# Query and key transfers of a hybrid decoder's mixer: transfers with an outermost DRAM dimension of two replaced by transfers of 32 or 64 rows

## The chip, the core and the metric

One core of a Trainium2 chip runs the whole program. The metric is device microseconds of one execution, as the median of several runs; less is better.

## What is computed

Two decoder layers over 512 tokens of width 1024, all in float32. Each layer is a half-step SwiGLU FFN, a token mixer and a second half-step FFN, each followed by a layer norm. The mixer makes one input projection, hands its columns to three groups of heads, and projects their outputs back:

```python
aq, ak, av, bq, bk, bv, cc = jnp.split(x @ w_in[l], IN_SPLIT_IDX, axis=-1)
...
o_a = diff_attention(rope(aq), rope(ak), av, lam)      # 6 heads, two 32-wide score maps each
...
o_b = dilated_attention(rope(bq), rope(bk), bv)        # 6 heads of width 64
...
o_c, v_first = rwkv7_mixer(cc, ...)                    # 4 heads, a scan over the tokens
mix = jnp.concatenate([o_a, o_b, o_c], axis=-1) @ w_out[l]
x = layer_norm(DEEPNORM_ALPHA * x + mix, ...)
```

## The kernel before

Every large product is made of three matmuls of rounded halves (hi times hi, hi times lo, lo times hi), so that TensorE (PE) carries most of the time. The FFNs run over tiles of 128 tokens and 512 columns, with weights streamed through a ring (lines 70 to 87). The change lies in the mixer, which runs once in each of the two layers, from about 390 to 860 us and from about 1536 to 2010 us of the profiled execution.

In the mixer some twenty generators each write one strand of the work. A planner (`Board`, lines 369 to 479) keeps a modelled time for each engine and merges the strands: it always takes the strand whose next step is ready by the model, in the order of a list of ranks, and so sets the order of the instructions on every engine. The engines then work through their queues in that order. Its model gives a DMA issued by GpSimd (POOL) 1.04 us on POOL, and then the time of the bytes and 2 us more. Nothing in the model depends on the shape of a transfer. Most mixer instructions carry line 511, the line of the planner's wrapper, so they are told apart by the names of their tiles.

The strands that matter here:

- `columns` computes the input projection in 13 parts (p<-wh,xhi, p<-wl,xhi, p<-wh,xlo, 128x256). It is ready early and long, and the planner fills PE with it where attention isn't ready; below it is called the filler.
- `weights` loads the raw columns (wr, by SyncE), rounds them on ScalarE (wh) and subtracts on POOL (wl); eight wh and eight wl tiles hold two parts.
- `turner` transposes the rotated queries and keys (m<-kept,rc), splits them into hi and lo (z) and stores them to DRAM: qkA and qkB, three tensors each, one for a pair of heads, laid out as [hi or lo, q or k, 128 channels, 512 tokens].
- `fetch` (line 766) brings one head after another back into SBUF, by POOL's DMAs. A head takes two tiles, q and k, of four such slots, so two heads are in flight, and the next head's transfers wait for the last scores of the head before the last. The first head of each group also loads the group's bias tile, for which there is one slot: group B's waits until VectorE (DVE) has read A's for the last time.
- `attend` makes the scores of one head in four units of 128 queries (A: two matmuls p<-k,q each, on 96 rows; B: p<-q on 128 rows and p<-k,q on 64), then softmax on DVE and ScalarE (ACT), transposes (m<-kept,t) and products with the values (r<-v,aT).
- `inside`, `invert`, `scan` and `rwkv_out` do the RWKV heads, with many small matmuls of 64 or 32 columns.

A head of group A (heads are numbered pair, half) needs 96 rows of 4 KB in each tile, in q the rows hi, lo, hi and in k the rows hi, hi, lo. Rows 0 to 63 came by one transfer per tile, with a DRAM pattern of two by 32 rows: outermost step 256*S for q, and step 0 for k, which reads the same rows twice. Rows 64 to 95 came by a transfer of 32 rows. A head of group B took q's 128 rows by two transfers of two by 64 rows of 2 KB, and k2 by one of 64 rows.

Of the kernel before, what the change touches and what calls it, by code (L numbers as in the profile page):

```python
# [16 lines left out]
S = 512  # L17
# [349 lines left out]
HALF = [slice(0, 64), slice(64, 128)]  # L367
# [153 lines left out]
class Mix:  # L521
# [247 lines left out]
    def fetch(self):  # L769

        dma = self.gps.dma_start
        ap = lambda t, off, dims: bass.AP(tensor=t.tensor, offset=t.offset + off, ap=dims)
        for grp in "AB":
            for hp in range(3):
                for e in range(2):
                    yield f"qk{grp}{hp}", "x", "x"
                    if (hp, e) == (0, 0):
                        yield f"qk{grp}{hp}", "x", "x", "bias"
                        self.bias = self.get("bias", "bias")
                        dma(self.bias, self.tr.consts[:, 130:642] if grp == "A" else self.tr.consts[:, 642:1154])  # L780
                    a = self.get("x", "q", (128, 2, S))
                    d = self.qk[grp, hp]
                    hi, lo, k = e * 64 * S, (256 + e * 64) * S, 128 * S
                    if grp == "A":
                        b = self.get("x", "k", (128, 2, S))
                        dma(a[0:64], ap(d, hi, [[256 * S, 2], [2 * S, 32], [1, 2 * S]]))
                        dma(b[0:64], ap(d, hi + k, [[0, 2], [2 * S, 32], [1, 2 * S]]))
                        dma(a[64:96], ap(d, hi, [[2 * S, 32], [1, 2 * S]]))
                        dma(b[64:96], ap(d, lo + k, [[2 * S, 32], [1, 2 * S]]))
                    else:  # L790
                        b = self.get("x", "k2", (64, S))
                        dma(a[:, 0, :], ap(d, hi, [[256 * S, 2], [S, 64], [1, S]]))
                        dma(a[:, 1, :], ap(d, hi + k, [[0, 2], [S, 64], [1, S]]))
                        dma(b, ap(d, lo + k, [[S, 64], [1, S]]))
                    self.qkt[grp, hp, e] = a.bitcast(FR), b.bitcast(FR)
                    self.mark(f"q{grp}{hp}{e}")
# [753 lines left out]
```

## Time and profile before

| | |
|---|---|
| median of 3 runs | 2329.84 us (2324.28 to 2331.13) |
| the profiled execution, its own time | 2319.83 us |
| its span, first to last instruction | 2318.0 us |
| PE busy | 2215.6 us, 96% of the span |
| DVE, ACT, POOL busy | 1146.8, 803.4, 317.5 us |
| mean granted TensorE clock | 0.975 of 2.4 GHz |
| chain of waits that ended last: PE, DVE, DMA | 80%, 8%, 5% |

The page puts the busy time of each engine, its waits, the granted clock and the DMA queues beside each other. The waits of PE tell which transfers or engines it stood still for. The granted clock of a stretch tells at which of its two levels (1.2 and 2.4 GHz) the matmuls in it ran: 0.50 is the lower one, 1.00 the upper.

### The profile page before, as it was taken

To read this page: it belongs to the slowest core of one execution; us is meant where nothing else is said; L and a number is where in the kernel's file an instruction comes from. 1 tells how busy PE (TensorE), PEld (TensorE's weight loads), DVE (VectorE), ACT (ScalarE), POOL (GpSimd) and SP (SyncE) were. 2 spreads that over 40 slices of the span, in tenths; PEclk is the share of its full clock that TensorE was granted. 3 is DMA by queue.
4 is the path that set the end of the run, shared out by engine and by line. 5 is a ranking of instruction groups with operands and counts; after the bars stand their busy time and mean duration, and the time that the engine had idled before them with its cause. 6 is when DMAs were issued, how large, how long until landed. Compare 5 with 4: busy or idle time off the path is not lost.

```text
span 2318.0 us, 31736 instructions
## 1 busy us (share of the span) xinstructions
PE 2215.6 (96%) x12384; PEld 1863.6 (80%) x12384; DVE 1146.8 (49%) x2483; ACT 803.4 (35%) x1559; POOL 317.5 (14%) x344
## 2 busy tenths in 40 slices
PE   9999999988899999999999999999878999999998
PEld 8888888787776788888888888887877867888886
DVE  3333346766566633333653332656765666333336
ACT  4322223435444323222433222343444443222222
POOL 1000002343232200000010000033432322000000
PEclk9999999999899999999999999999987999999999
DMA  5333344354433323332543333432553323233334
GB/s 171 101 102 98 113 137 146 102 136 98 104 106 101 118 74 94 98 99 91 173 120 108 101 96 109 155 128 85 136 108 94 107 95 119 84 98 91 100 109 154
DMA packets 253030, 258.34 MB, mean 111 GB/s; under 512 B 45562, under 2 KB 202304, under 8 KB 252880
## 3 DMA queue, kind: packets, MB, share of 16 engines
q1 hardware_dynamic: 221488, 228.20, 32.4%
q0 software_dynamic: 30816, 27.06, 4.8%
q8 instruction: 97, 1.59, 0.3%
q10 hardware_dynamic: 576, 1.05, 0.1%
q14 instruction: 53, 0.43, 0.1%
HBM read 233.85 MB, written 22.28 MB: 110 GB/s over the span
## 4 chain that ended last, share of the span: by engine, by line
PE 80%; DVE 8%; DMA 5%; issue 4%; POOL 1%; ACT 1%; SPq 0%; POOLq 0%; DVEq 0%; ACTq 0%
PE p L87 18%; PE p L86 18%; PE p L85 18%; PE p L511 13%; PE m L511 4%; PE r L511 3%; DMA k<-qkA 3%; PE r L86 2%; PE r L85 2%; PE r L87 2%; DMA k<-qkB 1%; DVE x L511 1%; POOL wl L511 1%; DMA q<-qkB 0%; DVE x L146 0%
## 5 line engine op out<-in xcount | busy, mean ns | idle before, releaser
L80 DVE TENSOR_TENSOR lo<-raw,hi 128x1024 fp32r<-128x1024 f32 x300 | 366.2, 1223 | 627.8 <-ACT hi L79 627.5
L87 PE MATMUL p<-xhi,lo 128*128 128x512 f32 (+1 forms) x1392 | 535.7, 385 | 0.0
L86 PE MATMUL p<-xlo,hi 128*128 128x512 f32 (+1 forms) x1392 | 533.7, 383 | 0.7 <-DVE xlo L126 0.7
L85 PE MATMUL p<-xhi,hi 128*128 128x512 f32 (+1 forms) x1392 | 533.6, 383 | 0.5 <-ACT xhi L125 0.5
L79 ACT CAST hi<-raw 128x1024 fp32r<-128x1024 f32 x300 | 315.6, 1053 | 583.5 <-PE p L86 258.1
L86 PEld LDWEIGHTS p<-xlo,hi 128*128 128x128 f32 x1392 | 261.7, 188 | 56.3 <-DVE xlo L126 1.1
L85 PEld LDWEIGHTS p<-xhi,hi 128*128 128x128 f32 x1392 | 261.8, 188 | 53.8 <-ACT xhi L125 1.0
L87 PEld LDWEIGHTS p<-xhi,lo 128*128 128x128 f32 x1392 | 261.9, 188 | 52.6
L511 POOL TENSOR_TENSOR wl<-wr,wh 128x512 fp32r<-128x512 f32 x152 | 203.8, 1360 | 670.1 <-ACT wh L511 629.3
L511 PE MATMUL p<-wh,xhi 128*128 128x256 f32 (+1 forms) x704 | 233.7, 332 | 1.4 <-DVE rb L511 1.1
L511 PE MATMUL p<-wh,xlo 128*128 128x256 f32 (+1 forms) x704 | 218.9, 311 | 0.5 <-DVE xlo L511 0.4
L511 PE MATMUL p<-wl,xhi 128*128 128x256 f32 (+1 forms) x704 | 218.5, 310 | 0.0
L87 PE MATMUL p<-hi,hl 128*128 128x512 f32 x528 | 205.8, 390 | 0.0
L86 PE MATMUL p<-lo,hh 128*128 128x512 f32 x528 | 205.8, 390 | 0.0
L85 PE MATMUL p<-hi,hh 128*128 128x512 f32 x528 | 205.7, 390 | 0.0
L511 PEld LDWEIGHTS p<-wh,xhi 128*128 128x128 f32 x704 | 138.9, 197 | 12.7 <-PE p L511 1.5
L511 PEld LDWEIGHTS p<-wh,xlo 128*128 128x128 f32 x704 | 138.7, 197 | 7.6 <-DVE xlo L511 2.2
L246 DVE TENSOR_TENSOR hr<-p,hr 128x512 f32<-128x512 f32 x88 | 60.8, 691 | 167.3 <-PE p L87 156.9
L511 PEld LDWEIGHTS p<-wl,xhi 128*128 128x128 f32 x704 | 139.2, 198 | 4.3
L247 ACT CAST hh<-hr 128x512 fp32r<-128x512 f32 x88 | 54.3, 617 | 205.9 <-DVE hr L246 195.8
L511 ACT ACTIVATE t<-t,nm 128x128 f32<-128x128 f32 (+3 forms) x144 | 80.2, 557 | 125.0 <-DVE nm L511 124.0
L85 PEld LDWEIGHTS p<-hi,hh 128*128 128x128 f32 x528 | 99.1, 188 | 20.6
(253 smaller groups left out, 3061.0 us busy)
## 6 DMA issues: line engine op xcount, KB each, us to landing
raw<-in_ffn_a_down SPq DMA_DIRECT2D x66, 512.0 KB, 3.3
raw<-in_ffn_b_down SPq DMA_DIRECT2D x66, 512.0 KB, 3.3
raw<-in_ffn_a_gate SPq DMA_DIRECT2D x44, 512.0 KB, 3.8
raw<-in_ffn_a_up SPq DMA_DIRECT2D x44, 512.0 KB, 3.9
raw<-in_ffn_b_gate SPq DMA_DIRECT2D x40, 512.0 KB, 3.9
raw<-in_ffn_b_up SPq DMA_DIRECT2D x40, 512.0 KB, 3.8
wr<-in_w_in SPq DMA_DIRECT2D x56, 256.0 KB, 3.1
wr<-in_w_in SPq DMA_DIRECT2D x24, 512.0 KB, 3.8
```

The source lines that it names most:

```text
L79: nc.scalar.copy(hi, raw)
L80: (vec or nc.vector).tensor_tensor(lo, raw, hi.bitcast(FT), op=OP.subtract)
L85: mm(out, lh, rh, start=first, stop=False)
L86: mm(out, lh, rl, start=False, stop=False)
L87: mm(out, ll, rh, start=False, stop=last)
L246: nc.vector.tensor_tensor(hr, acc[1, f], hr, op=OP.mult)
L247: nc.scalar.copy(hi, hr)
L511: return call(*args, **kw)
```

## The change

In group A each of the two transfers of 64 rows becomes two of 32 rows, so that a head takes six transfers of 32 rows in the place of four. In group B each of the two transfers of 128 rows becomes two of 64, so that a head takes five in the place of three. Bytes and destinations stay as they are. For 12 heads in two layers that is 48 DMAs more on POOL's queue.

```diff
                     if grp == "A":
                         b = self.get("x", "k", (128, 2, S))
-                        dma(a[0:64], ap(d, hi, [[256 * S, 2], [2 * S, 32], [1, 2 * S]]))
-                        dma(b[0:64], ap(d, hi + k, [[0, 2], [2 * S, 32], [1, 2 * S]]))
-                        dma(a[64:96], ap(d, hi, [[2 * S, 32], [1, 2 * S]]))
-                        dma(b[64:96], ap(d, lo + k, [[2 * S, 32], [1, 2 * S]]))
+                        for n, (q, r) in enumerate(((hi, hi), (lo, hi), (hi, lo))):
+                            rows = slice(32 * n, 32 * n + 32)
+                            dma(a[rows], ap(d, q, [[2 * S, 32], [1, 2 * S]]))
+                            dma(b[rows], ap(d, r + k, [[2 * S, 32], [1, 2 * S]]))
                     else:
                         b = self.get("x", "k2", (64, S))
-                        dma(a[:, 0, :], ap(d, hi, [[256 * S, 2], [S, 64], [1, S]]))
-                        dma(a[:, 1, :], ap(d, hi + k, [[0, 2], [S, 64], [1, S]]))
+                        for rows, q in zip(HALF, (hi, lo)):
+                            dma(a[rows, 0, :], ap(d, q, [[S, 64], [1, S]]))
+                            dma(a[rows, 1, :], ap(d, hi + k, [[S, 64], [1, S]]))
                         dma(b, ap(d, lo + k, [[S, 64], [1, S]]))
```

The planner prices each added DMA at 1.04 us of POOL and so merges the strands in another order, on all engines and in both layers alike. Three places of the first layer show how.

POOL's queue at the fetch of group B's first pair of heads, before (bias, q and k are the tiles that the DMAs fill, wl the rounded remainders of the weights):

```order
L511 TENSOR_TENSOR wl<-wr,wh 128x512 x4
L511 DMA bias<-in_constants 128x512
L511 DMA q<-qkB_0_2687 128x1x512 x2
L511 DMA k_5615<-qkB_0_2687 64x512
L511 DMA q<-qkB_0_2687 128x1x512 x2
L511 DMA k_5620<-qkB_0_2687 64x512
L511 TENSOR_TENSOR wl<-wr,wh 128x512 x8
```

and after:

```order
L511 TENSOR_TENSOR wl<-wr,wh 128x512 x8
L511 DMA bias<-in_constants 128x512
L511 DMA q<-qkB_0_2687 64x512 x4
L511 DMA k_5604<-qkB_0_2687 64x512
L511 DMA q<-qkB_0_2687 64x512 x4
L511 DMA k_5611<-qkB_0_2687 64x512
L511 TENSOR_TENSOR wl<-wr,wh 128x512 x4
```

Each head has two transfers more, and four subtractions of weights have moved from behind the fetch to ahead of it.

PE's queue at the first two units of head (1,0) of group A, before (p<-wh,xlo and p<-wh,xhi are filler; the numbers behind p only count tiles):

```order
L511 MATMUL p_4492<-wh,xlo 128x256
L511 MATMUL p_4539<-k,q 128x256
L511 MATMUL p_4545<-k,q 128x256
L511 MATMUL m<-kept,t 128x128 x3
L511 MATMUL r<-v,aT 128x64 x2
L511 MATMUL p_4492<-wh,xhi 128x256
```

and after:

```order
L511 MATMUL p_4591<-wh,xlo 128x256
L511 MATMUL r<-t_4302,x_4306 32x32 x16
L511 MATMUL r<-t16t,x_4306 32x32 x16
L511 MATMUL p_4643<-k,q 128x256
L511 MATMUL p_4649<-k,q 128x256
L511 MATMUL m<-kept,t 128x128 x3
L511 MATMUL r<-v,aT 128x64 x2
L511 MATMUL p_4676<-k,q 128x256
L511 MATMUL p_4682<-k,q 128x256
```

Between the last scores of head (0,1) and these first ones there were 24 filler matmuls and three batches of the RWKV inversion, and now there are 54 and four. In return the second unit follows the first without the 12 filler matmuls that stood between them.

PE's queue at the start of group B, before:

```order
L511 MATMUL r<-v,aT 128x64 x4
L511 MATMUL m<-uv,am 64x64 x4
L511 MATMUL r<-t16t,x_4449 32x32 x16
L511 MATMUL p_5753<-q 128x256
L511 MATMUL p_5753<-k_5615,q 128x256
L511 MATMUL p_5761<-q 128x256
L511 MATMUL p_5761<-k_5615,q 128x256
L511 MATMUL m<-uv,am 64x64
```

and after:

```order
L511 MATMUL r<-uv,am 64x64
L511 MATMUL r<-st,kr 64x64
L511 MATMUL p_5790<-q 128x256
L511 MATMUL p_5790<-k_5604,q 128x256
L511 MATMUL p_5798<-q 128x256
L511 MATMUL p_5798<-k_5604,q 128x256
L511 MATMUL r<-zs,t16t 64x64 x4
L511 MATMUL m<-uv,am 64x64
```

From the last scores of group A to these first ones of group B there were 24 filler matmuls, and now there are 72. In return the eight units of B's first two heads, among which 48 filler matmuls were spread, now have none.

## Rows read from the trace of the kernel before

**Rows 1.** The page: busy us, share of the span and instructions, by engine.
```profile
PE 2215.6 (96%) x12384; PEld 1863.6 (80%) x12384; DVE 1146.8 (49%) x2483; ACT 803.4 (35%) x1559; POOL 317.5 (14%) x344
```

**Rows 2.** PE's waits, whole span: us in total, times, longest.
```profile
PE p L511 <- DMA k<-qkA: 38.7, 6, 11.5
...
PE p L511 <- DMA q<-qkB: 1.7, 2, 1.2
```

**Rows 3.** PE's timeline at score matmuls: start, us; in brackets the idle time before.
```profile
506.02 0.76 PE L511 MATMUL p<-k,q 96*128 96x256 f32 x2 [3.50 <-DMA k<-qkA]
...
545.05 0.77 PE L511 MATMUL p<-k,q 96*128 96x256 f32 x2 [8.60 <-DMA k<-qkA]
...
588.54 0.77 PE L511 MATMUL p<-k,q 96*128 96x256 f32 x2 [6.03 <-DMA k<-qkA]
...
630.72 0.55 PE L511 MATMUL p<-q 128*128 128x256 f32 x1 [1.23 <-DMA q<-qkB]
```

**Rows 4.** POOL's timeline at fetches: start, us of the issues; in brackets POOL's wait.
```profile
492.56 0.69 POOL L511 DMA_DIRECT2D q<-qkA  x1 [1.57 <-issue]
...
526.40 0.72 POOL L511 DMA_DIRECT2D q<-qkA  x1
...
574.15 0.70 POOL L511 DMA_DIRECT2D q<-qkA  x1
...
618.06 0.59 POOL L511 DMA_DIRECT2D bias<-in_constants  x1 [12.11 <-DVE r L511]
618.78 1.63 POOL L511 DMA_DIRECT2D q<-qkB  x2
620.38 0.59 POOL L511 DMA_DIRECT2D k<-qkB  x1
```

**Rows 5.** Single DMAs: size, us to landing (issued at 618.06, 618.78 and 494.42).
```profile
bias<-in_constants POOLq DMA_DIRECT2D x1, 256.0 KB, 2.8
...
q<-qkB POOLq DMA_DIRECT2D x1, 256.0 KB, 11.6
...
k<-qkA POOLq DMA_DIRECT2D x1, 128.0 KB, 11.4
```

**Rows 6.** POOL's DMA queue, 707 to 711 and 721 to 724 us: packets, MB, share.
```profile
q0 software_dynamic: 163, 0.37, 25.5%
...
q0 software_dynamic: 303, 1.11, 98.5%
```

**Rows 7.** The page: reloads of x by POOL, count, size, median us to landing.
```profile
x<-x POOLq DMA_DIRECT2D x8, 512.0 KB, 4.3
```

**Rows 8.** Filler, then eight stretches after waits: window, length, PE busy (instructions), granted clock, DMA.
```profile
496.00:500.00 4.00, 4.00 (x36) 1.00 0.92 184
...
506.00:512.00 6.00, 5.98 (x38) 0.74 0.45 69
545.00:553.00 8.00, 7.95 (x65) 0.68 0.20 61
588.50:597.00 8.50, 8.46 (x62) 0.65 0.09 26
628.00:644.00 16.00, 14.77 (x91) 0.57 0.21 56
1658.60:1665.00 6.40, 6.34 (x39) 0.73 0.43 70
1700.70:1709.00 8.30, 8.29 (x60) 0.61 0.14 46
1743.80:1757.00 13.20, 13.18 (x86) 0.58 0.10 31
1785.00:1801.00 16.00, 15.76 (x98) 0.57 0.23 55
```

**Rows 9.** 40 us of group B: PE, PEld, DVE, ACT, POOL busy, granted clock, DMA, GB/s.
```profile
700.00:740.00 40.00, 35.88 (x217) 27.05 (x216) 27.26 (x129) 20.80 (x74) 9.61 (x14) 1.00 0.38 123
```

**Rows 10.** What POOL waited for, 480 to 720 us.
```profile
POOL wl L511 <- ACT wh L511: 102.4, 11, 28.1
```

## The prediction

> **What bounds the kernel now.** I read the busy times first: PE works in 96% of the span [rows 1], so time can only come out of PE's own standing still, or out of its clock. Next come PE's waits, longest in total first. At the head stands not an engine but a transfer: the keys of group A, 38.7 us in six waits of up to 11.5 us, and with the queries of group B 40.4 us [rows 2]. PE's timeline places them: three A waits in each layer, at the first scores of a head. In the first layer PE came to them at 502.5, 536.5, 582.5 (A) and 629.5 us (B) and went on at 506.0, 545.1, 588.5 and 630.7 [rows 3]. POOL's timeline shows the other end: the transfers of these heads were issued from 492.56, 526.40, 574.15 and 618.78 [rows 4], so they landed 12 to 18 us after the first issue. A last look goes to the granted clock behind each wait: 0.57 to 0.74 over the next 6 to 16 us, where plain filler runs at 1.00 [rows 8]. PE comes back from standing still at 1.2 GHz. A stretch of length L at mean clock c loses L times (1 - c): behind the six A waits 1.6 + 2.6 + 3.0 + 1.7 + 3.2 + 5.5 = 17.6 us, at the two starts of group B 6.9 + 6.9 = 13.8 us. So about 72 us hang on these places, and no more than that is to be had.
>
> **Why these transfers are slow.** Two transfers of 256 KB were issued by POOL within a microsecond of each other: the bias, 128 rows, landed in 2.8 us, and the first one of group B, with its two outermost, in 11.6 us [rows 5]. Size and queue are the same, the pattern differs. The queue's share says what the pattern does: with two such transfers under way it kept 25.5% of sixteen engines busy, which is 4.1 engines, and moved 0.37 MB in 4 us; with plain 128-row transfers 98.5% and 1.11 MB in 3 us [rows 6]. So each transfer with a two outermost has run on two engines. The plain transfers of 32 rows behind them landed no sooner, 11.4 us [rows 5], as they share those engines. The Trainium skill says the same in "DMA: Bandwidth & Descriptors", section "Why a DMA increments its semaphore by 16 and not by 1": the count of engines is the largest up to 16 that divides the slowest dimension of both sides; the trace agrees, with 4.1 engines for two transfers.
>
> **The change part by part.** *Landing.* Six transfers of 32 rows (A) or five of 64 (B) have 32 or 64 outermost. How long one takes has no row of its own. From below the bias row bounds it, 2.8 us; the reloads of x, six large transfers in a row, 4.3 us [rows 7], are the nearest row for several in flight; from above it is 11.4 us, nothing gained. I take 4 us after the last issue, near the reloads.
>
> *Issue.* A plain issue holds POOL for 0.59 us [rows 4]. Group A's six take 3.5 us, so the heads land 3.5 + 4 = 7.5 us after the first issue: at 500.1, 533.9 and 581.7, and PE came at 502.5, 536.5 and 582.5 [rows 3, 4]. Group B's four q transfers take 2.4 us where two took 1.63, so the last issue ends at about 621.7 and lands at 625.7; PE came at 629.5. All four waits go: slack 2.4, 2.6, 0.8 and 3.8 us in the old order. The new order adds to it: filler costs 4.00/36 = 0.11 us per matmul [rows 8], and 18 more of them stand ahead of the first head, 30 ahead of head (1,0), 48 ahead of group B, which is 2.0, 3.3 and 5.3 us. So the landing may come as late as 4 us after what I took before the first two wait again. Gain: 40.4 us.
>
> *Clock.* Where PE doesn't stand still it doesn't come back slow. I take the 17.6 us behind the A waits whole. At the start of group B the clock was low for another reason too: many matmuls of 64 and 32 columns, and a wait for ACT; of its 13.8 us I take half, 6.9.
>
> *What POOL pays.* 48 issues of 0.59 us are 28 us on an engine that is busy 14% [rows 1], and nothing waits for them where POOL is idle. Two places could. The four subtractions that moved ahead of B's bias take about 5 us, under a POOL wait of 12.11 us for the bias slot [rows 4], so they are covered if their inputs are there. In group A the issues for head (1,1) now stand directly behind those of (1,0) and wait for the scores of head (0,1); behind them are queued the subtractions for the filler and the products for the RWKV inversion. They come some 7 us after those scores, and PE has 54 filler matmuls (6 us), four batches of inversion and three units of attention to do first.
>
> *What the new order gives back.* The total of PE's work is the same; filler moved ahead is missing later. Group B's first eight units now have none. A bare stretch of group B had PE busy for 35.9 of 40 us, at full clock [rows 9]; the new bare stretch is some 20 us, so 2 us in each layer. Three units of head (1,0) are bare too: 1 us. As the order is new on all engines and none of its other waits can be read in this trace, I take 5 us for each layer instead of 3, with 0 and 10 as ends: 10 us.
>
> **The sum.** 40.4 + 17.6 + 6.9 - 10 = 55 us. The profiled execution took 2319.8 us (1.8 us around its span), so it would take 2265. The median of the runs shown is 10.0 us above it, which I keep: 2275 us.
>
> **The rivals.** *B's bare start stays slow.* From 628 to 644 us PE ran at clock 0.57 [rows 8] where little filler stood between small matmuls. Now all of some 24 us is like that. Then the 6.9 us don't come back, and 8 us more in each layer run at 0.57, which is 7 us: gain 41, 2289 us. Against it: the bare stretch at 700 to 740 ran at 1.00 [rows 9]; for it: that stretch has no RWKV steps of 64 columns among it as this one has.
>
> *Everything comes back.* No wait anew, and all of the 13.8 us: 40.4 + 31.4 = 72, 2258 us.
>
> *The transfers stay slow.* If the two engines were not the cause, the last issue comes about 1 us later and only the order helps: each A wait gets shorter by the filler ahead of it (2.0, 3.3, little for the third), less 1 us, and 5 us for each layer are given back. That is a few us either way, 2325 us. Against it are the bias row and the queue's share [rows 5, 6]. A rule of the skill speaks for it: the same page, "Rules for kernel authors", says of two transfers to disjoint halves of the partitions "Don't bother — they serialize", as both use the same sixteen engines. By that rule nothing is gained; the trace has the transfers on two engines each, where there is something to win.
>
> *Slower: the weights queue behind the fetches.* The fetch of a head is 768 KB, and 0.37 MB a microsecond [rows 6] makes 2.1 us in which it has all sixteen engines, 4.2 us for two heads. A weight load that comes then waits that long. If each of the 24 fetches cost PE 4.2 us, 100 us would be lost against 55 won: 2375 us. It decides only where a load is late by more than the weights' lead. wh and wl hold two parts, so one of 96 matmuls, about 11 us, lies ahead; no wait of PE for wl is among the large ones [rows 2], and POOL spent 102.4 of 240 us waiting to be given wh [rows 10], so it is not POOL that would be late.
>
> **How the numbers follow.** The forecast has 0.62, B's slow start 0.20, everything back 0.07, slow transfers 0.06, late weights 0.05. The range takes in the first three: from 2256, where all 72 us come, to 2302, where the slow start (14 us) and the upper end of the give-back (10 us) come together, with 3 us for the spread of the runs. Within 0.3%, 7 us, a measurement of this kernel can't be told from no change: faster 0.90, same 0.05, slower 0.05.
>
> **What would show it.** In the profile after: q and k land 3 to 5 us after their issue; no waits of PE for them above 2 us; granted clock 1.00 at the first scores of A's heads; the weights' loads as fast as before. Landings above 8 us prove the transfer part wrong; a clock near 0.6 through B's first heads is the first rival; PE waiting for wl is the last. If q and k are off PE's list and the time still falls by less than 30 us, the part on the order was wrong.

## The result and the profile after

The changed kernel takes 2345.47 us in the median of 19 runs, the kernel before 2329.84 us in as many: ratio 1.0059, interval 1.0035 to 1.0082. It is slower by about 16 us where 55 us less was forecast. The profiled execution has a span of 2347.2 us.

Two views give a first account: the span with the mean granted clock, and PE's busy time. Here both stand for the changed kernel (before: 2318.0 us, 0.975 and [rows 1]).

```profile
core 0: 2347.2 us, clock 0.950
PE 2272.1 (97%) x12384; PEld 1902.4 (81%) x12384; DVE 1140.5 (49%) x2483; ACT 804.5 (34%) x1559; POOL 326.5 (14%) x392
```

PE stands still for 2347.2 - 2272.1 = 75.1 us, before for 2318.0 - 2215.6 = 102.4 us: 27 us less. The clock costs 2347.2 x 0.050 = 117 us, before 2318.0 x 0.025 = 58 us: 59 us more. The difference, +32 us, is about the 29 us between the spans. So waits were won and clock was lost, and the page's row of the granted clock (40 slices of the span, in tenths) shows where:

```profile
PEclk9999999999876899999999999999997779999999
```

The low digits stand in the slices from 587 to 821 us and again from 1760 to 1936 us, in the mixer of each layer from the end of group A on.

**The transfers did what was forecast.** The page's DMA issues (size, median us from issue to landing) for queries, keys and raw weight columns:

```profile
wr<-in_w_in SPq DMA_DIRECT2D x56, 256.0 KB, 3.3
q<-qkB POOLq DMA_DIRECT2D x48, 128.0 KB, 4.1
q<-qkA POOLq DMA_DIRECT2D x36, 128.0 KB, 4.7
k<-qkA POOLq DMA_DIRECT2D x36, 128.0 KB, 4.7
```

Against 11.4 to 11.6 us [rows 5] they land in 4.1 to 4.7. With two of the old transfers under way the queue kept 4.1 of sixteen engines busy and moved 0.37 MB in 4 us [rows 6]. Now, with split ones under way from 697 to 700 us (packets, MB, share), it keeps 94.2% of them busy, which is 15.1:

```profile
q0 software_dynamic: 271, 0.76, 94.2%
```

The queue's packets changed too: 30816 before and 10080 now for 27 MB, and those that are gone are of under 512 bytes. As the queue's share of the engines' time in the whole span only fell from 4.8% to 4.0%, they are a small part of its work; what they added to the 11 us is not shown apart. The waits of [rows 2] are gone from PE's list, whose first rows now are all waits for engines (us in total, times, longest):

```profile
PE m L511 <- DVE xlo L511: 17.4, 8, 5.1
PE m L511 <- DVE t L511: 8.6, 8, 1.6
PE p L511 <- DVE xlo L511: 4.9, 2, 2.5
```

PE's timeline shows the first scores of head (1,0), before them in [rows 3] 8.60 us of waiting, now none:

```profile
545.09 0.51 PE L511 MATMUL p<-k,q 96*128 96x256 f32 x2
```

**The clock was lost behind group A.** The table of windows cuts the first layer's mixer at its score matmuls into five stretches: group A, group B's pairs one, two and three, and from the last B score to the next transposes of x. Columns: window, length, busy us (instructions) of PE, PEld, DVE, ACT, POOL, then granted clock, DMA share, GB/s. Before:

```profile
506.00:631.20 125.20, 105.31 (x1063) 98.69 (x1064) 82.85 (x288) 64.12 (x218) 41.47 (x47) 0.90 0.45 107
631.20:684.60 53.40, 50.71 (x390) 43.19 (x389) 31.80 (x132) 20.08 (x67) 12.31 (x12) 0.86 0.31 91
684.60:703.70 19.10, 17.95 (x131) 13.69 (x130) 12.56 (x51) 14.48 (x49) 8.59 (x9) 1.00 0.40 119
703.70:718.30 14.60, 13.18 (x77) 9.92 (x77) 9.50 (x49) 9.85 (x39) 2.09 (x4) 1.00 0.37 118
718.30:779.40 61.10, 56.87 (x291) 43.37 (x290) 40.64 (x132) 17.58 (x46) 21.10 (x21) 1.00 0.30 92
```

and after:

```profile
510.20:619.50 109.30, 102.51 (x986) 95.27 (x984) 82.88 (x290) 62.65 (x215) 46.52 (x61) 0.98 0.48 133
619.50:671.30 51.80, 49.01 (x385) 40.13 (x384) 27.25 (x109) 19.64 (x60) 12.81 (x16) 0.69 0.25 78
671.30:705.70 34.40, 32.04 (x182) 24.04 (x181) 16.02 (x82) 16.35 (x58) 7.63 (x12) 0.75 0.24 70
705.70:725.80 20.10, 20.10 (x90) 15.64 (x90) 8.36 (x42) 9.99 (x36) 1.12 (x2) 0.50 0.14 53
725.80:797.40 71.60, 66.94 (x298) 50.71 (x298) 40.66 (x130) 17.97 (x46) 20.11 (x20) 0.84 0.23 74
```

Group A is 16 us shorter, as wanted: PE's standing still falls from 19.9 to 6.8 us, and the clock from a loss of 12.5 us (125.2 x 0.10) to 2.2 us. Then four stretches run at 0.69, 0.75, 0.50 and 0.84, where before the last three ran at 1.00. They lose 16.1 + 8.6 + 10.1 + 11.5 = 46 us, before 7.5 us. Part of the longer third and fourth stretch is work that has moved there (182 matmuls for 131, and 90 for 77), but the sum of the five is 287.2 us, where it was 273.4. The second layer repeats it: 109.1, 50.5, 34.4, 20.1 and 71.6 us at 0.98, 0.72, 0.75, 0.50 and 0.84.

Finer windows over the start of group B, same columns:

```profile
616.00:620.00 4.00, 4.00 (x44) 3.32 (x43) 1.81 (x10) 0.27 (x1) 0.00 (x0) 1.00 0.73 203
620.00:624.00 4.00, 4.00 (x28) 2.71 (x27) 0.98 (x6) 1.89 (x7) 0.00 (x0) 0.78 0.00 0
624.00:652.00 28.00, 28.00 (x203) 22.66 (x204) 12.05 (x52) 13.01 (x41) 3.80 (x3) 0.50 0.06 18
```

PE shows no idle time in these 36 us. The clock falls where the filler ends (the last one starts at 618.30 us) and scores, transposes, products with the values and RWKV matmuls of 64 and 32 columns follow alone until 644.35 us. It is back at 1.00 from 656 us, behind more filler, falls again at about 670 us, at the end of a wait of 2.45 us for xlo, and lies at 0.50 from 696 to 728 us.

### The profile page after: what moved, and what is told of

Same layout as the page of the kernel before. It is cut to its first block, busy times and chain, and to the rows that moved or that the text cites. A ratio compares the mean times of both kernels' runs of the same rounds, so it can differ in the third digit from the quotient of the medians.

```text
span 2347.2 us, 31808 instructions
## 1 busy us (share of the span) xinstructions
PE 2272.1 (97%) x12384; PEld 1902.4 (81%) x12384; DVE 1140.5 (49%) x2483; ACT 804.5 (34%) x1559; POOL 326.5 (14%) x392
## 3 DMA queue, kind: packets, MB, share of 16 engines
q0 software_dynamic: 10080, 26.94, 4.0%
## 4 chain that ended last, share of the span: by engine, by line
PE 88%; DVE 9%; ACT 2%; issue 1%; DMA 0%; POOL 0%; SPq 0%; DVEq 0%; ACTq 0%
PE p L87 18%; PE p L86 18%; PE p L85 18%; PE p L511 17%; PE r L511 6%; PE m L511 5%; PE r L87 2%; PE r L86 2%; PE r L85 2%; DVE x L511 1%; DVE t L511 1%; DVE xlo L511 0%; DVE x L146 0%; DVE rs_t L511 0%; DVE l L511 0%
## 5 line engine op out<-in xcount | busy, mean ns | idle before, releaser
L87 PEld LDWEIGHTS p<-hi,hl 128*128 128x128 f32 x528 | 99.2, 188 | 20.5
L86 PEld LDWEIGHTS p<-lo,hh 128*128 128x128 f32 x528 | 99.2, 188 | 20.4
```

Of the source, the lines that this page charges most:

```text
L86: mm(out, lh, rl, start=False, stop=False)
L87: mm(out, ll, rh, start=False, stop=last)
```

## Experiments

In the first four, transfers and order are taken apart. A kernel's `raw` DMA is issued but not told to the planner; `note` tells the planner of a DMA without issuing it. With that, either form of the transfers can run in either order.

**Split transfers in the order of before** (fast_old_order), as a difference to the changed kernel; the same is done for group B:

```diff
+                    raw, note = self.nc.gpsimd.dma_start, lambda *aps: self.board.note("pool", "dma_start", aps, 1.04)
...
+                        note(a[0:64], ap(d, hi, [[256 * S, 2], [2 * S, 32], [1, 2 * S]]))
+                        note(b[0:64], ap(d, hi + k, [[0, 2], [2 * S, 32], [1, 2 * S]]))
+                        note(a[64:96], ap(d, hi, [[2 * S, 32], [1, 2 * S]]))
+                        note(b[64:96], ap(d, lo + k, [[2 * S, 32], [1, 2 * S]]))
...
-                            dma(a[rows], ap(d, q, [[2 * S, 32], [1, 2 * S]]))
-                            dma(b[rows], ap(d, r + k, [[2 * S, 32], [1, 2 * S]]))
+                            raw(a[rows], ap(d, q, [[2 * S, 32], [1, 2 * S]]))
+                            raw(b[rows], ap(d, r + k, [[2 * S, 32], [1, 2 * S]]))
```

> The transfers of 32 and 64 rows, with the planner told of the old ones, so that every engine but POOL has the order of the kernel before; on POOL only the split transfers differ. Theory (the split transfers gain, the new order loses through PE's clock): q and k land after 4 to 5 us, the 40 us of waits for them are gone, PE's clock behind them is 1.00, and the run takes 40 to 60 us less than before, 2270 to 2290 us. Rival (the split transfers themselves cost, by taking all sixteen engines from the weights): no faster than before, 2330 us or more, with new waits for wl or wr.

Measured: 2258.30 us, ratio 0.9714 (0.9679 to 0.9750), 67.5 us below the kernel before, which was run beside it (2325.82). That is 12 us better than the range expected. PE's 12384 matmuls stand in the same order in this trace and in that of the kernel before, so the gain is that of the transfers.

```profile
core 0: 2254.2 us, clock 0.986
PE 2194.2 (97%) x12384; PEld 1846.5 (82%) x12384; DVE 1137.7 (50%) x2483; ACT 802.9 (36%) x1559; POOL 329.3 (15%) x392
```

By the account above: 60.0 us of standing still (before 102.4) and 2254.2 x 0.014 = 32 us of clock (before 58). The two gains, 42 and 26 us, make 68; the two spans differ by 64 (2318.0 and 2254.2), the medians by 67.5. Its B stretches beside those of the changed kernel:

```profile
607.30:659.00 51.70, 49.01 (x390) 42.03 (x389) 32.36 (x133) 20.29 (x68) 13.07 (x16) 0.90 0.33 98
659.00:677.80 18.80, 17.75 (x132) 13.63 (x131) 12.36 (x51) 14.18 (x47) 8.69 (x11) 1.00 0.41 120
677.80:691.50 13.70, 12.96 (x79) 9.88 (x78) 9.76 (x50) 10.08 (x40) 2.75 (x6) 1.00 0.39 126
691.50:751.50 60.00, 56.85 (x290) 43.16 (x289) 39.54 (x132) 17.57 (x46) 19.96 (x20) 1.00 0.29 88
```

**The old transfers in the new order** (slow_new_order): the reverse edit, the split ones noted and the old ones issued raw.

```diff
+                            note(a[rows], ap(d, q, [[2 * S, 32], [1, 2 * S]]))
+                            note(b[rows], ap(d, r + k, [[2 * S, 32], [1, 2 * S]]))
+                        raw(a[0:64], ap(d, hi, [[256 * S, 2], [2 * S, 32], [1, 2 * S]]))
+                        raw(b[0:64], ap(d, hi + k, [[0, 2], [2 * S, 32], [1, 2 * S]]))
```

> The transfers of before with the order of the changed kernel: the planner is told of the new transfers, the old ones are issued. Theory: slower than the changed kernel or like it, 2345 to 2375 us, with the low clock in group B as there, and some of the waits for k back. Rival (the split transfers cost, the order is harmless): faster than before, below 2325 us.

Measured: 2380.17 us, 1.0241 (1.0207 to 1.0274), 5 us above the range expected. PE's list has the transfers again, and the third pair of group B runs as in the changed kernel (the windows' columns as above):

```profile
PE p L511 <- DMA k<-qkA: 21.8, 5, 10.0
715.90:735.80 19.90, 19.90 (x90) 15.48 (x89) 8.50 (x43) 9.99 (x36) 1.13 (x2) 0.50 0.16 57
```

The four cells, each as the difference of its median to that of the kernel before that was run beside it:

| | old transfers | split transfers |
|---|---|---|
| old order | 0 | -67.5 us |
| new order | +54.4 us | +15.6 us |

The split is worth 67 us in the old order and 39 in the new. The new order costs 54 us with the old transfers and 83 with the split ones. The changed kernel's time is these two, and the second is the larger. The low clock of the third pair comes with the new order, whichever the transfers. Between the traced executions of the changed kernel and of fast_old_order PE stands still 15 us more (75.1 and 60.0) and the clock costs 85 us more (117 and 32); the spans differ by 93. So the order's cost is the clock for the greater part.

**One group alone, in the old order** (a_only, b_only): fast_old_order with the split of the other group taken back. Here for group B, which leaves a_only:

```diff
-                        for rows, q in zip(HALF, (hi, lo)):
-                            raw(a[rows, 0, :], ap(d, q, [[S, 64], [1, S]]))
-                            raw(a[rows, 1, :], ap(d, hi + k, [[S, 64], [1, S]]))
+                        raw(a[:, 0, :], ap(d, hi, [[256 * S, 2], [S, 64], [1, S]]))
+                        raw(a[:, 1, :], ap(d, hi + k, [[0, 2], [S, 64], [1, S]]))
```

> The order of before, and only group A's transfers split (group B's stay two by 64 rows). Theory (the gain is PE's waits for a transfer and the slow clock behind them, place by place): group A's six waits, 38.7 us, and the 17.6 us of clock behind them go, 2265 to 2275 us, some 50 to 58 us below before. Rival (the gain of 67 us with both split comes from engines set free for all other transfers): half of it or less for either group alone, 2290 us or more here.

> The order of before, and only group B's transfers split. Theory: the waits for q and k in group B are 2 us, and some of the slow clock at its start goes, at most 14 us in two layers: 2312 to 2326 us. Rival (engines set free): 2300 us or less.

Measured: group A alone 2290.19 us, 0.9828 (0.9784 to 0.9873); group B alone 2314.71 us, 0.9927 (0.9897 to 0.9957). B came out as expected, and not as its rival had it. A is 15 us above its range, at the very figure of its rival (2290), though none of the waits for k of [rows 2] is left. The rows of its two layers, from the third B pair on, show where the time went (same columns; layer one, then layer two):

```profile
683.90:700.50 16.60, 15.60 (x78) 12.05 (x77) 10.20 (x51) 10.15 (x40) 2.48 (x4) 0.82 0.32 104
700.50:774.10 73.60, 70.23 (x290) 54.40 (x290) 40.59 (x128) 17.86 (x45) 21.02 (x21) 0.76 0.25 77
...
1828.40:1842.90 14.50, 13.18 (x79) 9.93 (x78) 9.64 (x50) 10.10 (x40) 2.32 (x4) 1.00 0.39 120
1842.90:1906.50 63.60, 60.55 (x291) 46.28 (x290) 39.59 (x132) 17.56 (x46) 18.29 (x17) 0.92 0.25 79
```

The same instructions in the same order took 90.2 us in one layer and 78.1 in the other, by the clock alone: PE stands still for 4.4 us in either. So the old order, too, can lose the clock there; what decides it is not shown.

**Dense work added at B's start.** If the clock is what the order costs, then matmuls that do nothing should pay for themselves. In the changed kernel each score unit of group B (dense_b), or of its first pair alone (dense_pair0), gets four matmuls more, whose result the real scores overwrite.

```diff
+                    for _ in range(4 if hp == 0 else 0):
+                        self.nc.tensor.matmul(sc[:, :nn], a[:, 0, qs], a[:, 1, :nn], start=True, stop=True)
                     pe.matmul(sc[:, :nn], a[:, 0, qs], a[:, 1, :nn], start=True, stop=False)
```

> The changed kernel with each first score matmul of group B made five times over (four extra, overwritten by the last; 192 extra matmuls of 256 to 512 columns in two layers, some 29 us at full clock), in the same order. Theory (group B loses because PE's work there is too sparse for the clock to come back): the clock in group B rises from 0.5 to near 1.00 and the run gets no slower or faster than the changed kernel, 2310 to 2345 us. Rival (the order's chains of dependent steps cost, and the clock only follows): slower than the changed kernel by the added work, 2365 to 2375 us.

> The changed kernel with the four extra score matmuls only for the first pair of heads of group B (eight units in a layer, some 5 us of added work at full clock), in the same order. Theory (with no filler among these units PE's work is too sparse, and the clock falls there without any wait): the clock from B's first score to the second pair of heads is 1.00 instead of about 0.6, that stretch of 52 us takes 45 us in spite of the added work, and the run takes 5 to 15 us less than the changed kernel, 2330 to 2340 us. Rival (chains of dependent steps set the pace there): the stretch and the run get 5 us longer in each layer, 2355 us.

Measured: dense_b 2342.67 us, 1.0062 (1.0037 to 1.0087) against before; dense_pair0 2335.52 us, 1.0025 (0.9999 to 1.0051). The first pair's stretch in dense_pair0, and the third pair's, which got nothing:

```profile
616.40:660.60 44.20, 40.77 (x414) 33.86 (x413) 28.72 (x109) 19.23 (x59) 12.86 (x16) 0.98 0.31 90
...
692.00:711.60 19.60, 19.60 (x90) 15.28 (x89) 8.49 (x43) 9.97 (x36) 1.12 (x2) 0.51 0.14 54
```

With 28 of the 32 added matmuls in it (the first four stand just ahead), the stretch takes 44.2 us where it took 51.8, at 0.98 for 0.69; in layer two 43.4 for 50.6, at 0.99 for 0.72. So the bare start loses its clock for want of dense work, and that costs 7 to 8 us a layer net of the added work. Against the runs of before beside it dense_pair0 stands at +6 us, where the changed kernel is at +16. dense_b, with the work added in all three pairs, stands at +17. Its third pair (layer one, then two):

```profile
702.90:724.30 21.40, 21.40 (x119) 17.38 (x118) 7.99 (x39) 10.11 (x37) 1.11 (x2) 0.71 0.13 50
1868.50:1886.10 17.60, 17.60 (x119) 14.22 (x118) 7.88 (x39) 10.02 (x37) 1.11 (x2) 0.89 0.18 61
```

With some 30 matmuls more it takes 21.4 and 17.6 us, where it took 20.1. The clock rises there too, but not to the 1.00 that was expected, and over the kernel the added work costs what it wins.

**The same in the fast kernel** (fast_dense_start): fast_old_order with four added matmuls for each unit of head (0,0) of group B.

```diff
+                    for _ in range(4 if (hp, e) == (0, 0) else 0):
+                        self.nc.tensor.matmul(sc[:, :nn], a[:, 0, qs], a[:, 1, :nn], start=True, stop=True)
```

> Split transfers in the order of before, with the four extra score matmuls for the first head of group B alone (four units in a layer, 2.4 us of added work), where that kernel's clock still falls to 0.74 over 20 us. Theory: the clock stays at 1.00 there, 5 us come back in each layer for 2.4 us paid, 2250 to 2256 us against 2258. Rival (what falls there falls for another reason): 2260 to 2264 us.

Measured: 2259.36 us, 0.9696 (0.9656 to 0.9735). That is between its two ranges. The interval lies over that of fast_old_order (0.9679 to 0.9750), so no gain can be told from none. From 600 to 620 us the clock is 1.00 where fast_old_order has 0.74, but that stretch loses only 5 us in all (51.7 x 0.10), and the added work takes its own time. Of these two kernels, dense work that does nothing paid only in the one where the loss was large.

**Dense work behind the first pair too** (dense_rwkv): dense_pair0, and eight more matmuls before each output step of the RWKV heads.

```diff
+            for _ in range(8):
+                self.nc.tensor.matmul(y[0].rearrange("p j d -> p (j d)"), tr.ident, tr.ident, start=True, stop=True)
```

> Edit: the changed kernel with dense_pair0's four added score matmuls ahead of each score unit of group B's first pair, and besides eight added 128x128 matmuls ahead of each output step of the RWKV heads (their results are overwritten). The second part is some 13 us of added PE work in each layer, which stands among the small matmuls behind B's first pair. Theory, the low clock behind the first pair (8 + 10 + 10 us lost in a layer of the changed kernel) comes from sparse, small matmuls there, and dense work brings it back: the last B pair's stretch falls from 20.1 to 14 to 15 us, what the clock costs in a layer from about 28 (dense_pair0) to under 12 us, and the time is 2325 to 2340 us in spite of 26 us of added work. Rival, the clock there is not moved by work of its own kind: the added 26 us come on top of dense_pair0's 2336, about 2360 us, with the last pair still at 20 us and 0.50.

Measured: 2331.35 us, 1.0005 (0.9978 to 1.0033), as the first theory had it and 29 us below the rival. The third pair in the two layers:

```profile
700.70:720.10 19.40, 19.40 (x91) 15.11 (x90) 8.52 (x43) 10.01 (x36) 1.12 (x2) 0.53 0.15 55
...
1860.70:1872.20 11.50, 11.50 (x90) 8.88 (x89) 7.78 (x41) 9.03 (x35) 1.12 (x2) 1.00 0.26 93
```

Layer two has the clock back, and 90 matmuls take 11.5 us instead of 20.1. Layer one has not, with the same order. None of the added matmuls lies in this stretch; the nearest two batches of eight end 12 and 7 us ahead of it. From the end of the first of them (688.94 and 1849.00 us) to the stretch PE's rows are alike in the two layers to 0.05 us, and the clock is at 1.00 in both. So what PE did in the 12 us ahead does not tell at which clock the stretch runs. The two rows also measure the account by L times (1 - c): it gives a loss of 9.1 us for layer one, and the difference is 7.9.

**A standstill made on purpose** (pause_old_order): fast_old_order with one wait of PE ahead of the first scores of B's third pair, while ScalarE copies a tile onto itself twelve times.

```diff
+                    if x["id"] == (2, 0, 0):
+                        self.nc.tensor.matmul(sc[:, :128], tr.ident, tr.ident, start=True, stop=True)
+                        for _ in range(12):
+                            self.nc.scalar.copy(sc[:, :128], sc[:, :128])
```

> Edit: fast_old_order (split transfers, the order of the kernel before) with one standstill of PE made in each layer, ahead of the first scores of B's last pair: a matmul writes the score tile, ScalarE copies it onto itself twelve times (some 3 us), and only then may the scores be written. The two pauses themselves cost 2 x 3 = 6 us. Theory, a short standstill where no filler is left is enough to put the clock at 0.50 through the work behind it: the stretch from there to the last B score goes from 13.7 us plus the pause to about 20 us plus the pause, the tail behind it loses some us too, and the time is 2275 to 2290 us (6 us of pause and 10 to 25 us of clock on top of 2258). Rival, a standstill costs itself and a few us of clock at most, and the low clock of the changed kernel in its last pairs has another cause (its own kind of work there): 2262 to 2270 us.

Measured: 2278.96 us, 0.9796 (0.9768 to 0.9823), 49 us below the runs of before beside it, where fast_old_order is 67.5 below: 18 us for two pauses. That is in the theory's range, but the profiled execution speaks for the rival: it was the fastest of five, 2266.85 us, and in it the two pauses cost themselves and little clock. PE's wait for them, and the third pair behind:

```profile
PE p L511 <- ACT p L1256: 8.0, 2, 4.0
679.80:695.90 16.10, 15.37 (x79) 11.62 (x78) 9.49 (x49) 9.38 (x35) 1.12 (x2) 0.83 0.19 66
```

16.1 us at 0.83 is 2.4 us more than without the pause, not the 6 us of a stretch at 0.50. The other four executions took 2277.8 to 2283.9 us at a mean clock of 0.978 to 0.980, the profiled one 0.985; 0.006 of 2280 us is 14 us, about the difference between them. So in the traced execution two standstills cost their 8 us and little clock. The other four lie above every execution of fast_old_order (2252 to 2267 us), at a lower mean clock, so there the standstills cost clock too; where, no trace shows.

**The planner's price for a DMA.** The order comes from one number, 1.04 us for a DMA issued by POOL. The changed kernel was run with five others; the profile has an issue at 0.59 us [rows 4].

```diff
-                cost = {"pool": 1.04, "act": 0.5, "sp": 0.47}[self.name]
+                cost = {"pool": 0.70, "act": 0.5, "sp": 0.47}[self.name]
```

> The changed kernel with the planner's price of a POOL DMA at 0.59 us, as measured, in the place of 1.04. By the planner's order 894 filler matmuls of 256 columns stand ahead of group B (960 in the changed kernel, 882 before) and 54 stay among its first two heads (none, 48). Theory: the filler in group B keeps the clock up, and with the fast transfers the run takes 2265 to 2295 us. Rival (any order made for the split transfers loses in group B's chains): 2325 us or more.

> The changed kernel with the planner's price of a POOL DMA at 0.45 us. Filler matmuls of 256 columns ahead of group B: 882 (as before; the changed kernel 960), among the eight units of its first two heads: 42 (before 48, changed 0). Theory (the split transfers gain 67 us, and an order loses as much as PE's clock falls in group B where no filler lies among its units): 2255 to 2280 us. Rival (orders other than the old one lose by chance, filler or not): above 2300 us at two of these four prices or more, with the clock no guide to which.

> As before, the price at 0.70 us: 882 filler matmuls ahead of group B, 36 among its first eight units. Theory: 2255 to 2285 us. Rival: as for 0.45.

> The price at 0.80 us: 924 filler matmuls ahead of group B, 36 among its first eight units, but none after the sixth. Theory: between, 2275 to 2310 us, with a low clock from the seventh unit on at most. Rival: as for 0.45.

> The price at 0.90 us: 966 filler matmuls ahead of group B, more than in the changed kernel, but 66 among its first eight units, most of them in the second head. If it is the filler among the units that keeps the clock, the first two heads run at 1.00 but for the first four units, and the run takes 2265 to 2300 us. If it is the filler used up ahead of group B that costs, it is as slow as the changed kernel, 2330 us or more.

The filler counts are those of 128x256 matmuls in PE's queue ahead of group B's first score and among its first eight units. Where the trace has other counts in layer two, they stand behind the first:

| price | us | ratio to before | filler ahead, among |
|---|---|---|---|
| 0.45 | 2302.38 | 0.9894 (0.9837 to 0.9950) | 882, 42; 924, 12 |
| 0.59 | 2274.28 | 0.9789 (0.9743 to 0.9835) | 894, 54; 924, 42 |
| 0.70 | 2256.45 | 0.9706 (0.9646 to 0.9767) | 882, 36 |
| 0.80 | 2287.78 | 0.9847 (0.9785 to 0.9910) | 924, 36 |
| 0.90 | 2316.15 | 0.9926 (0.9884 to 0.9969) | 966, 66 |
| 1.04 (changed kernel) | 2345.47 | 1.0059 (1.0035 to 1.0082) | 960, 0 |
| order of before, split transfers | 2258.30 | 0.9714 (0.9679 to 0.9750) | 882, 48 |

From 0.70 upward the time rises with the price. The runs at 0.59, 0.70 and 0.80 lie in the ranges of their theories, 0.90 between its two. The rival to the filler asked for two of the four later prices above 2300 us, with the clock no guide to which. Two there are, 0.45 and 0.90, but the clock is a guide to them: the traced executions of 0.70, 0.80, 0.45 and 0.90 took 2258, 2290, 2311 and 2317 us at a mean clock of 0.986, 0.975, 0.969 and 0.964.

0.45 was a miss, and more in layer two: the five stretches take 260.3 and 278.7 us in its two layers, in fast_old_order 246.4 and 248.0. The planner gave its two layers different orders, which the expectation overlooked. The first pair with 42 filler matmuls among its units, and with 12:

```profile
609.70:650.20 40.50, 40.27 (x359) 35.35 (x358) 30.43 (x113) 18.67 (x61) 16.34 (x19) 1.00 0.43 125
1747.20:1805.30 58.10, 56.75 (x476) 47.55 (x475) 30.89 (x127) 19.65 (x63) 11.45 (x15) 0.72 0.26 78
```

In layer one the loss lies behind the last B score: 79.8 us at 0.87, with 376 matmuls where fast_old_order has 290 in 60.0 us, so part of it is work that has moved there.

At 0.90 the filler among the first units does keep the first pair's clock, 0.91 and 1.00 in the two layers. What it loses lies behind: its third pair takes 22.2 us at 0.50 in layer one and 13.2 us at 1.00 in layer two. So over these kernels the first pair ran at 0.85 to 1.00 with 36 filler matmuls or more among its first units, and at 0.72 or less with 12 or none, where nothing was added. For the pairs behind it the count is no guide, and what decides their clock is not settled by these runs. The price of 0.70 and the old order with split transfers are the best versions found, each some 67 us below the kernel before.

## Why the prediction was wrong

**What bounds the kernel, and the cause of the slow transfers: right.** In the old order the split brought 42 us of standing still and 26 us of clock by the traced executions; the prediction's terms were 40.4 and 17.6 + 6.9 = 24.5. The forecast of these, 65 us, met 67.5 between the medians. The two engines of a transfer with an outermost two are borne out by the landings of 4.1 to 4.7 us and by the 15.1 engines that are busy now. The Trainium skill's rule in "DMA: Bandwidth & Descriptors", section "Rules for kernel authors", that two transfers to disjoint halves of the partitions aren't worth it as both use the same sixteen engines, doesn't hold where the one transfer has an outermost dimension of two: the trace has 11.6 us for the whole and 4.1 for the halves.

**Landing and issue: right.** I took 4 us to landing; the rows have 4.1 to 4.7. None of the waits that were priced is left. POOL's added issues cost PE nothing visible: its waits for wl come to 2.9 us in the whole span, and to the same in slow_new_order, which lacks these issues.

**The clock behind A's waits: right.** The first layer's A stretch lost 12.5 us by it and now loses 2.2.

**What the new order gives back: the step that failed.** It stood in the sum with 10 us, ends 0 and 20 for both layers; the four cells give 83. That is the whole miss: 73 us too little here, less the 2.5 us by which the transfers were better, are the 70.5 us between 2275 and 2345.5. The term priced PE's standing still alone and put the clock of the bare stretches at 1.00, at no cost. The traces have it the other way round: some 15 us of standing still and 85 of clock. The sign that the prediction gave for this came: q and k are off PE's list, and the time has not fallen by 30 us. The full clock was read from [rows 9]: 40 us of group B at 1.00, which I called a bare stretch. It wasn't bare. The filler (128x256) is missing in it, but grouped by form that window of the kernel before has 38 output-projection matmuls of 128x512, 15.7 of its 35.9 busy us (columns: line, engine, operation, tile, shapes, count, busy us, mean ns, idle time ahead):

```profile
L511 PE MATMUL p<-wh,xhi 128*128 128x512 f32 x12 | 5.3, 443 | 0.0
L511 PE MATMUL p<-wh,xlo 128*128 128x512 f32 x13 | 5.3, 404 | 0.2 <-DVE xlo L511 0.2
L511 PE MATMUL p<-wl,xhi 128*128 128x512 f32 x13 | 5.1, 394 | 0.0
L511 PE MATMUL m<-uv,am 128*64 128x64 f32 x18 | 3.0, 246 | 0.4 <-DVE gb L511 0.4
L511 PE MATMUL m<-st,kr 64*64 64x64 f32 x17 | 2.9, 244 | 0.0
```

The last two lines are RWKV matmuls of 64 columns, so the prediction is also wrong in saying that the stretch has none among it.

In the changed kernel the same window has 13 of the 128x512:

```profile
L511 PE MATMUL p<-wh,xhi 128*128 128x512 f32 x4 | 2.5, 628 | 0.0
L511 PE MATMUL p<-wh,xlo 128*128 128x512 f32 x5 | 2.4, 487 | 0.0
L511 PE MATMUL p<-wl,xhi 128*128 128x512 f32 x4 | 1.8, 452 | 0.0
```

In group B's third pair (705.7 to 725.8 us) none of them is left, and 24 RWKV matmuls of 64 columns stand there instead; that pair runs at 0.50:

```profile
L511 PE MATMUL r<-uv,am 64*64 64x64 f32 x8 | 1.0, 330 | 0.0
L511 PE MATMUL r<-st,kr 64*64 64x64 f32 x8 | 0.9, 311 | 0.0
L511 PE MATMUL r<-zs,t16t 64*64 64x64 f32 x8 | 0.7, 324 | 0.0
```

Grouped by form, [rows 9] would not have carried the full clock over to a stretch without wide matmuls. It would not have given the size either: of the 38 only six lie in the third pair of the kernel before (703.7 to 718.3 us), which runs at 1.00.

**The first rival named the mechanism and the place.** B's bare start did stay slow: the first pair's stretch loses 16.1 us against 7.5 before, 8.6 us more a layer, where the rival had 3.5. What it lacked above all is the rest: the low clock went on through pairs two and three and the tail, 30 us a layer, where the order had moved dense work away too; that it was lost for this reason is shown for the first pair alone. Neither the forecast nor a rival looked beyond the first pair, though the prediction itself says that the order is new on all engines.

**New waits** are the smaller part: PE stands still for 75.1 us with the new order against 60.0 with the old, both with split transfers. Of these 15 us, 8.5 are waits for xlo (17.4 + 4.9 against 13.0 + 0.8) and 6 waits for t (8.6 against 2.6).

**The other rivals.** That the transfers stay slow is refuted by the landings. That the weights queue behind the fetches too: wr lands in 3.3 us, and PE waits 2.9 us for wl. That everything comes back (72 us less, 2258) is nearly what happens when the order is held: 67.5 us less. That 2258.30 was measured is luck, as the kernel before ran 4 us faster beside it than beside the changed kernel. Two readings are off without bearing on the sum: the slowest of the four fetches landed 18.7 us after its first issue (545.1 less 526.40), and 768 KB is the fetch of a head of group A, where one of group B has 640.

**Left open:** why a given order keeps or loses the clock behind B's first pair. With dense work added ahead of it the third pair ran at 1.00 in one layer of two, and so it did at the price of 0.90 with none added. The two standstills cost little clock in the one execution traced.

## What to carry to other kernels

When a change also alters what a planner sees, run the two apart before judging either: hold the order and change the transfers, then the other way round. The order, which hangs on one number in the planner, was worth more here (83 us) than the transfers (67 us). A stretch is bare only when its rows, grouped by form, say so. Dense matmuls that can run at any time are worth keeping for PE's stretches of small ones: at the start of group B they held the clock up, in the planner's orders and where they were added. Look at the order and the clock of every layer, as they need not be alike.

## What was not expected of the hardware

- The granted clock fell to 0.50 with PE recorded as busy for 28.00 of 28.00 us, where little but small matmuls stood. In the kernel before I had seen the low clock behind waits. The Trainium skill, in "TensorE: Matmul & The Clock Gate", section "Part 1", ties the low clock to an idle PE; these rows show none, but the ends of matmuls are modelled in them, so short gaps would not show.
- Matmuls that do nothing made a stretch shorter: with 28 more in it, 44.2 us instead of 51.8.
- The same instructions in the same order ran at different clocks in the two layers of one execution: 11.5 us at 1.00 and 19.4 us at 0.53, with the last 12 us ahead of them alike on PE.
